# Gates of chunk and memory attention projected with the activations stationary, and turned back on VectorE and by GpSimd's transfers

## The chip, the core and the metric

One core of one Trainium2 chip runs the whole program. TensorE (PE) multiplies, VectorE (DVE) and ScalarE (ACT) do elementwise work, GpSimd (POOL) and SyncE (SP) mostly issue DMAs. The metric is device time in microseconds for one execution, the median of the runs. The kernel before takes 915.07 us (three runs, 915.05 to 915.77).

## The reference

Two layers of one mixer each; 256 rows of width 2048, all in f32. One input projection feeds three groups of heads, each group's output is multiplied by a SiLU gate, and one output projection follows.

```python
h = x @ w_in
a_q, a_k, a_v, a_z, b_q, b_k, b_v, b_z, b_lr, m_q, m_z = jnp.split(h, cuts, axis=-1)
y_a = chunk_band_attention(...)      # 8 heads of 128
y_b = rms_norm(gla_chunk_recurrence(...))   # 4 heads of 128
y_m = memory_attention(...)          # 4 heads of 128 over 256 memory rows
y = jnp.concatenate([y_a * silu(a_z), y_b * silu(b_z), y_m * silu(m_z)], axis=-1)
out = y @ w_out
x = layer_norm(ALPHA * x + out, ln_g, ln_b)
```

`a_z` has 1024 columns, `b_z` and `m_z` 512 each. The change touches `a_z` and `m_z`.

## The kernel before, in words

Every projection is cut into groups of 512 weight columns (four of 388 for the values). A group's weights come in eight pieces of 512 KB, called here pieces 0 to 7. Each f32 operand is used as the sum of a high and a low part, both stored as float32r, and of the four products the low times low is left out. `piece` (L128) issues the DMA of a piece on SP's queue, then `parts` (L115) makes its high part `wh` with a cast on ACT (L117) and its low part `wl` with a subtraction on DVE (L118). The buffers `raw`, `wh` and `wl` have four slots each, so the cast of a piece waits until PE has read the piece four before it.

There are two ways to multiply a group.

- `ws_group` (L250) keeps the weights stationary and streams the activations: for 128 rows of the contraction and 128 columns one matmul of 512 (high and low activations side by side) and one of 256. The result stands with its columns on the partitions. `total` (L261) adds the two halves.
- `as_group` (L273) keeps the activations stationary and streams the weights: per 128 rows of the contraction and each half `t` of the 256 rows three matmuls of 512. The result stands with the rows on the partitions, in one accumulator `acc` of two halves.

In a layer the order of the groups is: memory keys and values, gated linear attention's queries and keys, the values, the queries and keys of chunk attention, memory's queries, then the gates: `G_BZ` (L857, `as_group`), `G_AZ0`, `G_AZ1`, `G_MZ` (L864 to L876, `ws_group`), then four groups of the output projection, called here out 0 to out 3 (L908 to L927, `as_group`). Out 0 reads its activations `yq` in this order: gated linear attention at pieces 0 and 1, chunk attention's first four heads at pieces 2 and 3, its second four at 4 and 5, memory attention at 6 and 7.

The heads are generators. `tick` (L46) runs a step of one of them after every few matmuls of a group, and `finish` (L62) runs them to their end, so the order of PE's and SP's instructions is that in which the code is written and ticked. ACT, DVE and POOL are put in order by the build's scheduler, which gives `piece` a high priority. All five engines then work through their own list strictly in that order.

`turned` (L506) is a transposition that PE has no part in: DVE transposes blocks of 32 by 32 (L510), POOL writes them to HBM (`home`, L512, 256 KB), and four more DMAs of POOL read them back with the blocks exchanged (L514, 64 KB each, into `pT` or `yT`). The heads use it for their softmax, and `gla_turned` for the output of gated linear attention. Attention's outputs `yraw[1]` to `yraw[3]` have their columns on the partitions, as the result of `ws_group` has.

In the loop over `G_AZ0`, `G_AZ1` and `G_MZ` each of a group's two accumulators goes through ACT's and DVE's addition (`total`), SiLU on ACT (L870), then, when the group's heads are done, the product with `yraw` on DVE (L874) and the split into high and low (`x`).

Of the kernel before, what the change touches and what calls it, by code (L numbers as in the profile page):

```python
# [8 lines left out]
F32 = mybir.dt.float32  # L9
# [9 lines left out]
P = 128  # L19
# [17 lines left out]
def hybrid_trunk_kernel(  # L37
# [35 lines left out]
    def enter(name, bufs=1, **kw):  # L73
        return ctx.enter_context(tc.tile_pool(name=name, bufs=bufs, **kw))
# [8 lines left out]
    sm = enter("sm", 1)  # L83
    psd = enter("psd", 2, space=bass.MemoryType.PSUM)
    psa = enter("psa", 4, space=bass.MemoryType.PSUM)
    drm = enter("drm", 3, space=bass.MemoryType.DRAM)

    uid = [0]

    def nm(s):  # L90
        uid[0] += 1
        return f"{s}_{uid[0]}"
# [7 lines left out]
    def scratch(shape, dtype=F32):  # L100
        return sc.tile(shape, dtype, name=nm("sc"), tag="sc")
# [18 lines left out]
    def load_quarter(src):  # L120

        with tc.high_priority(AHEAD):
            raw = wp.tile([P, 4, T], F32, name=nm("raw"), tag="raw")
            x = operand()
            sp.dma_start(raw, src)
            parts(x[0], x[1], raw)
        return x

    def piece(src, n, kp=2, home=None):

        with tc.high_priority(AHEAD):
# [12 lines left out]
        return hi, lo  # L144
# [125 lines left out]
        mm(o, xl[:, j, ts], wh[:, kk], False, False)  # L270
        mm(o, xh[:, j, ts], wl[:, kk], False, kt == 15)

    def as_group(src, xq, n, kp=2, first=None):  # L273

        acc = psd.tile([P, 2, 512], F32, name=nm("acc"), tag="acc")
        for pc in range(16 // kp):
            if first is not None and pc % 2 == 0:
                xq.append(load_quarter(first[pc // 2]))
            w = piece(src[pc], n, kp)
            for kk in range(kp):  # L280
                for t in range(2):
# [209 lines left out]
    def gla_turned(yraw, ng, y):  # L491

        yT = []
        for par in range(2):
            yT.append(hd.tile([P, 4, P], F32, name=nm("yT"), tag=("gq", "gk")[par]))
            turned(yT[par], yraw[:, 2 * par:2 * par + 2].rearrange("p t d -> p (t d)"), P)
            yield 6
        for par in range(2):
            for t in range(2):
                for b in range(2):  # L500
                    hi, lo = (x.rearrange("p k (t a j) -> p k t a j", t=2, j=32)[:, b * 2 + par, t] for x in y[:2])
                    src = yT[par].rearrange("p a (t b j) -> p t b a j", t=2, j=32)[:, t, b]
                    act.activation(hi, src, AF.Copy, scale=ng[:, 0:1])
                    dve.scalar_tensor_tensor(lo, src, ng[:, 0:1], hi.bitcast(F32), op0=ALU.mult, op1=ALU.subtract)
            yield 1

    def turned(dst, src, n):

        blocks = scratch([P, 4, n])
        dve.transpose(blocks.rearrange("p b (g j) -> p g b j", j=32), src.rearrange("p (g b j) -> p g b j", b=4, j=32))  # L510
        home = drm.tile([P, 4, n], F32, name=nm("home"), tag=f"home{n}")
        pool.dma_start(home, blocks)  # L512
        for b in range(4):
            pool.dma_start(dst[b * 32:(b + 1) * 32], home[:, b].rearrange("(a i) n -> i a n", a=4))  # L514

    SCALE = P ** -0.5

    def a_head(h, load_bias, bias, q, k, asv, y):

        if h + 2 < 8:  # L520
            load_bias(h + 2)
        pb = bank()
        mm(pb[:, 0:128], q[:, 0:128], k[:, 0:128], True, True)
        mm(pb[:, 128:384], q[:, 128:256], k, True, True)
        s = scratch([P, 384])
        dve.scalar_tensor_tensor(s, pb[:, :384], SCALE, bias[h], op0=ALU.mult, op1=ALU.add)  # L526
        mx = small([P, 2], "mx", 4)
        zs = small([P, 2], "zs", 4)
        own = (slice(0, 128), slice(128, 384))
        for t in range(2):  # L530
            dve.tensor_reduce(mx[:, t:t + 1], s[:, own[t]], AX.X, ALU.max, negate=True)  # L531
        for t in range(2):
            act.activation(s[:, own[t]], s[:, own[t]], AF.Exp, bias=mx[:, t:t + 1], accum_out=zs[:, t:t + 1])  # L533
        dve.reciprocal(zs, zs)
        for t in range(2):
            dve.tensor_scalar(s[:, own[t]], s[:, own[t]], zs[:, t:t + 1], None, op0=ALU.mult)
        pT = tp.tile([P, 4, 96], F32, name=nm("pT"), tag="pT")
        turned(pT, s, 96)
        yield 9
        po = bank()  # L540
        v0 = 528 + h * P
        pv, pov = pT.rearrange("p a (g j) -> p g a j", j=32), po[:, :256].rearrange("p (t a j) -> p t a j", t=2, j=32)
        mm(pov, asv[:, 0, v0:v0 + P], pv[:, 0:2], True, False)
        mm(pov[:, 1], asv[:, 1, v0:v0 + P], pv[:, 2], False, True)
        act.copy(y, po[:, :256])
        yield 2

    def m_head(h, q, mk, mv, y):

        pb = bank()  # L550
# [18 lines left out]
        turned(pT, s.rearrange("p t m -> p (t m)"), 128)  # L569
# [12 lines left out]
        act.copy(y, po[:, :256])  # L582
        yield 2
# [187 lines left out]
    for l in range(L):  # L771
# [77 lines left out]
        for i, a, b in ws_group(w512[l, G_MQ], xq):  # L849
# [4 lines left out]
        waiting.extend(gens[-1])  # L854


        acc = as_group([[w512[l, G_BZ, h * 4 + pc // 2][:, pc % 2 * 512:pc % 2 * 512 + 512] for h in range(2)]  # L857
                        for pc in range(8)], xq, 512)
# [4 lines left out]
        waiting[:0] = gens[0]  # L863
        for i, g in ((1, G_AZ0), (2, G_AZ1), (3, G_MZ)):  # L864
            y = operand()
            gates = []
            for j, a, b in ws_group(w512[l, g], xq):
                sz = scratch([P, 2, T])
                total(sz, a, b)
                act.activation(sz, sz, AF.Silu)  # L870
                gates.append((j, sz))
            finish(gens[i])
            for j, sz in gates:
                dve.tensor_tensor(sz, sz, yraw[i][:, j:j + 2], op=ALU.mult)  # L874
                parts(y[0][:, j:j + 2], y[1][:, j:j + 2], sz)
            yq.append(y)  # L876
        finish(gens[0])


# [4 lines left out]
        for n in range(WO_N):  # L884
# [9 lines left out]
            if last and n == WO_N - 1:  # L894
# [23 lines left out]

                norm_last(accs, rest, stats, gb, rows, more)
                break  # L920
            acc = as_group(src, yq, 512)
            for t in range(2):
                add_residual(n, t, acc[:, t], stats)
            if last:
# [91 lines left out]
```

## Time and profile before

| | |
|---|---|
| profiled execution, its own time | 914.58 us |
| span of its instructions | 912.8 us, granted clock 0.998 |
| PE, DVE, ACT, POOL busy | 905.3, 605.2, 489.5, 99.0 us |
| DMA | 191.43 MB, mean 210 GB/s |
| gates of layer 0: G_AZ0 begins, out 0 begins | 293.43 and 365.27 us |

The profile names tiles without their numbers, output first: `acc<-x,wh` is a matmul that streams the activations against stationary weights, `acc<-wh,x` one that streams the weights. A row of the timeline has the start, the duration, the engine, the line, the operation, its tiles and shape, and in brackets how long the engine had been idle and what ended that. Rows of groups have the count, the busy sum, the mean of one in ns, and the idle time before them. A row of waits has the sum, the count and the longest. The ends of matmuls are modelled, so the spacing of their starts is the better measure.

### The profile page before, as it was taken

How to read it: one execution, taken by the hardware profiler on the slowest of the kernel's cores; microseconds unless marked ns; L12 is line 12 of the kernel's file. 1: busy time of each engine (PE TensorE's matmuls, PEld its weight loads, DVE VectorE, ACT ScalarE, POOL GpSimd, SP SyncE). 2: the span in 40 equal slices, each digit the busy share in tenths (PEclk: the TensorE clock that was granted, in tenths of full speed). 3: DMA queues.
4: the chain of work that ended last, by engine and by line, in shares of the span. 5: the costliest groups of instructions: out<-in, count | busy, mean ns of one | idle time of the engine just before them, and what ended most of it. 6: DMA issues, size and time to landing. Idle time of an engine off the chain costs nothing.

```text
span 912.8 us, 14367 instructions
## 1 busy us (share of the span) xinstructions
PE 905.3 (99%) x5404; PEld 796.2 (87%) x5404; DVE 605.2 (66%) x861; ACT 489.5 (54%) x714; POOL 99.0 (11%) x189
## 2 busy tenths in 40 slices
PE   9999999999999999999999999999999999999997
PEld 7889998998888888888888899889888888888885
DVE  6764478656576767655587676885756576776566
ACT  6654475474454666433476445754844465763340
POOL 1000000013031232000000000001121232420000
PEclk9999999999999999999999999999999999999999
DMA  8965865558575769766775466556575766696652
GB/s 300 341 198 167 298 222 167 161 198 248 184 223 177 240 218 273 217 197 193 225 256 167 146 203 204 186 156 212 181 246 186 217 207 218 204 294 207 195 162 92
DMA packets 76822, 191.43 MB, mean 210 GB/s; under 512 B 9545, under 2 KB 33481, under 8 KB 76497
## 3 DMA queue, kind: packets, MB, share of 16 engines
q1 hardware_dynamic: 69120, 173.30, 58.8%
q0 software_dynamic: 7488, 16.96, 6.5%
q8 instruction: 42, 0.69, 0.3%
q10 hardware_dynamic: 144, 0.26, 0.1%
q14 instruction: 28, 0.22, 0.1%
HBM read 182.06 MB, written 8.39 MB: 209 GB/s over the span
## 4 chain that ended last, share of the span: by engine, by line
PE 98%; DMA 0%; DVE 0%; ACT 0%; SPq 0%; issue 0%
PE acc L95 90%; PE bk L95 8%; DMA raw<-w 0%; PE bk L601 0%; PE bk L397 0%; SPq L178 0%; ACT res L757 0%; ACT wh L117 0%; DVE stats L742 0%; PE bk L344 0%; DVE res L741 0%; DVE res L693 0%; DVE mvt L696 0%; SPq L165 0%; PE bk L745 0%
## 5 line engine op out<-in xcount | busy, mean ns | idle before, releaser
L118 DVE TENSOR_TENSOR wl<-raw,wh 128x1024 fp32r<-128x1024 f32 (+3 forms) x321 | 369.8, 1154 | 227.2 <-ACT wh L117 226.0
L117 ACT CAST wh<-raw 128x1024 fp32r<-128x1024 f32 (+3 forms) x321 | 318.9, 994 | 324.7 <-PE acc L95 237.6
L95 PE MATMUL acc<-x,wh 128*128 128x512 f32 x1248 | 396.1, 399 | 0.5 <-ACT wh L117 0.5
L95 PE MATMUL acc<-wh,x 128*128 128x512 f32 (+2 forms) x1236 | 356.7, 370 | 0.2 <-ACT wh L117 0.2
L95 PEld LDWEIGHTS acc<-x,wl 128*128 128x128 f32 x1248 | 234.4, 188 | 55.2
L95 PEld LDWEIGHTS acc<-wh,x 128*128 128x128 f32 x1236 | 227.3, 188 | 27.6 <-ACT wh L117 0.5
L95 PE MATMUL acc<-x,wl 128*128 128x256 f32 x1248 | 245.7, 278 | 0.0
L95 PE MATMUL acc<-wl,x 128*128 128x512 f32 (+2 forms) x618 | 227.9, 369 | 0.0
L95 PEld LDWEIGHTS acc<-x,wh 128*128 128x128 f32 x1248 | 192.2, 189 | 2.5 <-ACT wh L117 0.7
L95 PEld LDWEIGHTS acc<-wl,x 128*128 128x128 f32 x618 | 116.2, 188 | 14.7 <-DVE wl L118 0.4
L514 POOL DMA_DIRECT2D pT<-home x96 | 52.6, 554 | 54.6 <-DMA home<-sc 33.4
L512 POOL DMA_DIRECT2D home<-sc x28 | 15.7, 561 | 361.6 <-DVE sc L510 357.9
L533 ACT ACTIVATE sc<-sc,mx 128x128 f32<-128x128 f32 (+1 forms) x32 | 14.3, 449 | 18.0 <-DVE mx L531 18.0
L526 DVE SCALAR_TENSOR_TENSOR sc<-bk,bias 128x384 f32<-128x384 f32 x16 | 8.7, 543 | 11.7 <-PE bk L95 11.7
L386 ACT ACTIVATE sc<-sc 128x512 f32<-128x512 f32 x12 | 7.6, 633 | 14.7 <-DVE sc L384 14.6
L510 DVE STREAM_TRANSPOSE sc<-sc 128x384 f32<-128x384 f32 (+1 forms) x24 | 14.9, 619 | 0.5
L304 POOL DMA_DIRECT2D gwraw<-gate_w x6 | 3.1, 524 | 106.0 <-PE bk L589 105.2
L118 DVE TENSOR_TENSOR x<-sc,x 128x512 fp32r<-128x512 f32 x20 | 13.5, 685 | 0.7 <-ACT x L117 0.7
L634 DVE SCALAR_TENSOR_TENSOR res<-res,acc 128x512 f32<-128x512 f32 x15 | 9.7, 684 | 5.4 <-PE acc L95 5.4
L118 DVE TENSOR_TENSOR x<-res,x 128x512 fp32r<-128x512 f32 (+2 forms) x14 | 10.5, 765 | 4.2 <-ACT x L117 4.2
L95 PE MATMUL bk<-qk,qk 128*128 128x128 f32 (+1 forms) x64 | 13.1, 327 | 0.0
L118 DVE TENSOR_TENSOR x<-raw,x 128x1024 fp32r<-128x1024 f32 x5 | 6.1, 1212 | 10.5 <-ACT x L117 10.5
(207 smaller groups left out, 586.1 us busy)
## 6 DMA issues: line engine op xcount, KB each, us to landing
raw<-w SPq DMA_DIRECT2D x214, 512.0 KB, 4.2
raw<-w SPq DMA_DIRECT2D x64, 388.0 KB, 3.2
raw<-w SPq DMA_DIRECT2D x83, 256.0 KB, 3.5
bias<-relw SPq DMA_DIRECT2D x16, 192.0 KB, 4.3
home<-sc POOLq DMA_DIRECT2D x16, 192.0 KB, 3.1
pT<-home POOLq DMA_DIRECT2D x64, 48.0 KB, 3.8
home<-sc POOLq DMA_DIRECT2D x12, 256.0 KB, 4.0
res<-xT SPq DMA_DIRECT2D x4, 512.0 KB, 5.1
```

Of the source, the lines that this page charges most:

```text
L95: pe.matmul(o, l, r, start=start, stop=stop, skip_group_check=True)
L117: act.copy(hi, src)
L118: dve.tensor_tensor(lo, src, hi.bitcast(F32), op=ALU.subtract)
L304: pool.dma_start(raw[i * 16:i * 16 + 16], gate_w[l])
L386: act.activation(dd, dd, AF.Abs)
L510: dve.transpose(blocks.rearrange("p b (g j) -> p g b j", j=32), src.rearrange("p (g b j) -> p g b j", b=4, j=32))
L512: pool.dma_start(home, blocks)
L514: pool.dma_start(dst[b * 32:(b + 1) * 32], home[:, b].rearrange("(a i) n -> i a n", a=4))
L526: dve.scalar_tensor_tensor(s, pb[:, :384], SCALE, bias[h], op0=ALU.mult, op1=ALU.add)
L533: act.activation(s[:, own[t]], s[:, own[t]], AF.Exp, bias=mx[:, t:t + 1], accum_out=zs[:, t:t + 1])
L634: dve.scalar_tensor_tensor(r, r, ALPHA, acc, op0=ALU.mult, op1=ALU.add)
```

## The change

The three groups `G_AZ0`, `G_AZ1` and `G_MZ` now go through `as_group`. Their weights lie in HBM as two halves of 256 columns, so a piece is fetched with two DMAs of 256 KB, as `G_BZ`'s already were (`halves`). The result has the rows on the partitions: ACT applies SiLU straight from the accumulator, in two instructions (L889), and `turned` brings it to columns on partitions: two transpositions, two writes to HBM, then eight loads into `zT`. The new generator `gated` waits until the heads are done and multiplies `zT` with `yraw`, in four instructions (L517), and splits the products in two. It is put among the running generators, and `as_group` of out 0 finishes it before the piece that reads its result (`need`: at pieces 2, 4 and 6). `turned` now takes several tiles and issues all writes before the first load. The pause in `gla_turned` is 2 then 6 ticks in place of 6 and 6.

```diff
-    def as_group(src, xq, n, kp=2, first=None):
+    def as_group(src, xq, n, kp=2, first=None, need={}):
...
+            finish(need.get(pc, ()))
             w = piece(src[pc], n, kp)
...
+    def gated(zT, yraw, heads, y):
+
+        while not all(h in done for h in heads):
+            yield 1
+        for j in range(0, 4, 2):
+            gz = scratch([P, 2, T])
+            for t in range(2):
+                z, o, r = (zT[:, t].rearrange("p a (k j) -> p k a j", j=32)[:, j:j + 2],
+                           *(x[:, :, t * P:(t + 1) * P].rearrange("p k (a j) -> p k a j", j=32) for x in (gz, yraw[:, j:j + 2])))
+                dve.tensor_tensor(o, z, r, op=ALU.mult)
+            parts(y[0][:, j:j + 2], y[1][:, j:j + 2], gz)
+
+    def turned(n, *todo):
+
+        homes = []
+        for _, src in todo:
+            blocks = scratch([P, 4, n])
+            dve.transpose(blocks.rearrange("p b (g j) -> p g b j", j=32), src.rearrange("p (g b j) -> p g b j", b=4, j=32))
+            homes.append(drm.tile([P, 4, n], F32, name=nm("home"), tag=f"home{n}"))
+            pool.dma_start(homes[-1], blocks)
+        for (dst, _), home in zip(todo, homes):
+            for b in range(4):
+                pool.dma_start(dst[b * 32:(b + 1) * 32], home[:, b].rearrange("(a i) n -> i a n", a=4))
...
         for i, g in ((1, G_AZ0), (2, G_AZ1), (3, G_MZ)):
-            y = operand()
-            gates = []
-            for j, a, b in ws_group(w512[l, g], xq):
-                sz = scratch([P, 2, T])
-                total(sz, a, b)
-                act.activation(sz, sz, AF.Silu)
-                gates.append((j, sz))
-            finish(gens[i])
-            for j, sz in gates:
-                dve.tensor_tensor(sz, sz, yraw[i][:, j:j + 2], op=ALU.mult)
-                parts(y[0][:, j:j + 2], y[1][:, j:j + 2], sz)
-            yq.append(y)
+            acc = as_group(halves(g), xq, 512)
+            yq.append(operand())
+            zT = hd.tile([P, 2, 4, P], F32, name=nm("zT"), tag="qk", bufs=4)
+            sz = [scratch([P, 512]) for _ in range(2)]
+            for t in range(2):
+                act.activation(sz[t], acc[:, t], AF.Silu)
+            turned(P, *((zT[:, t], sz[t]) for t in range(2)))
+            need[i * 2] = [gated(zT, yraw[i], gens[i], yq[i])]
+            active.extend((x, now[0] + 5) for x in need[i * 2])
         finish(gens[0])
...
-            acc = as_group(src, yq, 512)
+            acc = as_group(src, yq, 512, need=need if n == 0 else {})
```

Three places in the programs, where the order on ACT, DVE and POOL differs. The first is ACT in layer 0 at the end of `G_MZ`. Before, with the operands of the last memory head (`sc<-pT`), the last pieces of `G_MZ` (`wh_3653`, `wh_3683`) and pieces 0 and 1 of out 0 (`wh_3720`, `wh_3738`):

```order
L117 CAST wh_3653<-raw_3652 128x1024
L117 CAST sc_3551<-pT_3356 128x2x128 x2
L117 CAST wh_3683<-raw_3682 128x1024
L262 ACTIVATE sc_3587<-acc_3478 128x512
L582 COPY yr_1035<-bk_3579 128x256
L870 ACTIVATE sc_3587<-sc_3587 128x512
L117 CAST wh_3720<-raw_3719 128x1024
```

Now `wh_3686`, `wh_3704`, `wh_3722`, `wh_3740` are pieces 0 to 3 of out 0, `sc_3542` is the operand of the last memory head, and `acc_3451` is the accumulator of `G_MZ`:

```order
L117 CAST wh_3686<-raw_3685 128x1024
L598 COPY yr_1035<-bk_3577 128x256
L117 CAST wh_3704<-raw_3703 128x1024
L117 CAST wh_3722<-raw_3721 128x1024
L117 CAST sc_3542<-pT_3363 128x2x128 x2
L598 COPY yr_1035<-bk_3631 128x256
L117 CAST wh_3740<-raw_3739 128x1024
L889 ACTIVATE sc_3660<-acc_3451 128x512
```

The last head's operand has moved from ahead of the last piece of `G_MZ` to behind piece 2 of out 0; PE's last products of that head (`bk_3631`) still stand ahead of piece 7 of `G_MZ`.

The second is DVE in layer 1, where the low parts of memory attention's gated output are written. Before, the last write (`x_7771`) is ahead of the low part `wl_8144`, piece 6 of out 0:

```order
L118 TENSOR_TENSOR wl_8108<-raw_8106,wh_8107 128x1024
L874 TENSOR_TENSOR sc_7998<-sc_7998,yr_5329 128x512
L118 TENSOR_TENSOR wl_8126<-raw_8124,wh_8125 128x1024
L118 TENSOR_TENSOR x_7771<-sc_7998,x_7771 128x2x256
L118 TENSOR_TENSOR wl_8144<-raw_8142,wh_8143 128x1024
```

Now `wl_8114` is piece 7 of out 0, `wl_8144` and `wl_8162` are pieces 0 and 1 of out 1, and `x_7928` is that output:

```order
L118 TENSOR_TENSOR wl_8114<-raw_8112,wh_8113 128x1024
L517 TENSOR_TENSOR sc_8066<-zT_7929,yr_5305 128x2x128
L517 TENSOR_TENSOR sc_8071<-zT_7929,yr_5305 128x2x128
L118 TENSOR_TENSOR wl_8144<-raw_8142,wh_8143 128x1024
L118 TENSOR_TENSOR gbrow_7953<-gbrow_7951,gbrow_7952 2x1024
L118 TENSOR_TENSOR wl_8162<-raw_8160,wh_8161 128x1024
L517 TENSOR_TENSOR sc_8066<-zT_7929,yr_5305 128x2x128
L517 TENSOR_TENSOR sc_8071<-zT_7929,yr_5305 128x2x128
L118 TENSOR_TENSOR x_7928<-sc_8066,x_7928 128x2x256
L118 TENSOR_TENSOR x_7928<-sc_8071,x_7928 128x2x256
```

The last write stood behind piece 5 of out 0 and now stands behind piece 1 of out 1, four pieces later. In layer 0 the two high casts (`x_3658` on ACT) stand behind `wh_3868`, the same piece 1 of out 1.

The third is POOL in layer 0 around the end of `G_MZ`. Before there are only the transfers of the heads, the gated linear attention's (`yT`) and the rows of the norm (`gb`, broadcasts of 256 KB):

```order
L514 DMA pT_3356<-home_3359 32x4x128 x4
L514 DMA yT_3458<-home_3461 32x4x128 x4
L890 DMA gb_4023<-ln_g 128x512
L891 DMA gb_4023<-ln_b 128x512
L820 MEMSET lr_5009 128x256
```

Now the gates' transfers stand between them (`zT_3430` of `G_AZ1`, `zT_3659` of `G_MZ`):

```order
L530 DMA zT_3430<-home_3437 32x4x128 x4
L530 DMA zT_3430<-home_3441 32x4x128 x4
L836 MEMSET lr_4985 128x256
L527 DMA home_3666<-sc_3664 128x512
L906 DMA gb_3999<-ln_g 128x512
L907 DMA gb_3999<-ln_b 128x512
L527 DMA home_3670<-sc_3668 128x512
L530 DMA zT_3659<-home_3666 32x4x128 x4
L530 DMA zT_3659<-home_3670 32x4x128 x4
```

Two broadcasts have come to stand between the two writes of `G_MZ`'s gates, and the loads follow both.

More of the change, by code (lines that the diff above doesn't have):

```diff
@@ L85, in hybrid_trunk_kernel @@
     psa = enter("psa", 4, space=bass.MemoryType.PSUM)
-    drm = enter("drm", 3, space=bass.MemoryType.DRAM)
+    drm = enter("drm", 6, space=bass.MemoryType.DRAM)
     uid = [0]
@@ L495, in gla_turned @@
             yT.append(hd.tile([P, 4, P], F32, name=nm("yT"), tag=("gq", "gk")[par]))
-            turned(yT[par], yraw[:, 2 * par:2 * par + 2].rearrange("p t d -> p (t d)"), P)
-            yield 6
+            turned(P, (yT[par], yraw[:, 2 * par:2 * par + 2].rearrange("p t d -> p (t d)")))
+            yield 2 + 4 * par
         for par in range(2):
@@ L505, in gla_turned @@
             yield 1
[L507 to L514, printed above, removed]
+    def gated(zT, yraw, heads, y):
[18 more added lines that the diff above has]
+                pool.dma_start(dst[b * 32:(b + 1) * 32], home[:, b].rearrange("(a i) n -> i a n", a=4))
     SCALE = P ** -0.5
@@ L537, in a_head @@
         pT = tp.tile([P, 4, 96], F32, name=nm("pT"), tag="pT")
-        turned(pT, s, 96)
+        turned(96, (pT, s))
         yield 9
@@ L568, in m_head @@
         pT = hd.tile([P, 4, 128], F32, name=nm("pT"), tag="qe" if h % 2 else "gb_")
-        turned(pT, s.rearrange("p t m -> p (t m)"), 128)
+        turned(128, (pT, s.rearrange("p t m -> p (t m)")))
         yield 7
@@ L854, in hybrid_trunk_kernel, with halves @@
         waiting.extend(gens[-1])
-        acc = as_group([[w512[l, G_BZ, h * 4 + pc // 2][:, pc % 2 * 512:pc % 2 * 512 + 512] for h in range(2)]
-                        for pc in range(8)], xq, 512)
+        def halves(g):
+            return [[w512[l, g, h * 4 + pc // 2][:, pc % 2 * 512:pc % 2 * 512 + 512] for h in range(2)] for pc in range(8)]
+        acc = as_group(halves(G_BZ), xq, 512)
         finish(gens[0])
@@ L863, in hybrid_trunk_kernel @@
         waiting[:0] = gens[0]
+        need = {}
         for i, g in ((1, G_AZ0), (2, G_AZ1), (3, G_MZ)):
-            y = operand()
-            gates = []
-            for j, a, b in ws_group(w512[l, g], xq):
-                sz = scratch([P, 2, T])
-                total(sz, a, b)
-                act.activation(sz, sz, AF.Silu)
-                gates.append((j, sz))
-            finish(gens[i])
-            for j, sz in gates:
-                dve.tensor_tensor(sz, sz, yraw[i][:, j:j + 2], op=ALU.mult)
-                parts(y[0][:, j:j + 2], y[1][:, j:j + 2], sz)
-            yq.append(y)
+            acc = as_group(halves(g), xq, 512)
[7 more added lines that the diff above has]
+            active.extend((x, now[0] + 5) for x in need[i * 2])
         finish(gens[0])
```

## The prediction

> **What bounds the kernel now.** I read the page first (busy times, the chain that ended last), then the waits, then the timeline of PE, ACT and POOL where the changed groups end.
>
> ```profile
> span 912.8 us, 14367 instructions
> ...
> PE 905.3 (99%) x5404; PEld 796.2 (87%) x5404; DVE 605.2 (66%) x861; ACT 489.5 (54%) x714; POOL 99.0 (11%) x189
> ...
> PE 98%; DMA 0%; DVE 0%; ACT 0%; SPq 0%; issue 0%
> ```
>
> PE is the whole chain. The waits say how little it is held up, and who waits for whom instead:
>
> ```profile
> ACT wh L117 <- PE acc L95: 237.6, 170, 2.1
> ...
> ACT wh L117 <- DMA raw<-w: 15.3, 20, 3.2
> ...
> PE bk L95 <- DVE eps L770: 1.1, 1, 1.1
> ...
> PE acc L95 <- ACT wh L117: 0.7, 2, 0.5
> ```
>
> ACT waits for PE to free a weight slot, seldom for a weight. So a microsecond of PE's work counts fully, and a wait of PE is never made up. The change is worth what it does to PE's rate, less any new wait of PE.
>
> **PE's rate: -3.1 us.** The end of the memory gates (weights stationary) and out 0 (activations stationary):
>
> ```profile
> 357.61 0.63 PE L95 MATMUL acc<-x,wh 128*128 128x512 f32 x2
> ...
> 364.57 0.63 PE L95 MATMUL acc<-x,wh 128*128 128x512 f32 x2
> ...
> 365.27 0.62 PE L95 MATMUL acc<-wh,x 128*128 128x512 f32 x2
> ...
> 381.60 0.62 PE L95 MATMUL acc<-wh,x 128*128 128x512 f32 x2
> ...
> 388.40 0.62 PE L95 MATMUL acc<-wh,x 128*128 128x512 f32 x2
> ```
>
> Both ways stream 1536 columns per step: twice 512 and twice 256, or thrice 512. From 357.61 to 364.57 are ten steps of 0.696 us, from 381.60 to 388.40 ten of 0.680. A group has 32 steps, so it goes from 22.27 to 21.76 us, and six groups give 6 x 0.51 = 3.1 us. A piece is four steps, 2.72 us. Out 0 begins at 365.27, which I call T0, and its piece 6 at 381.60, T0 + 16.33: then the memory gates' output must be there.
>
> **What the other engines pay: nothing, with cover.** Durations of one, by shape:
>
> ```profile
> L118 DVE TENSOR_TENSOR wl<-raw,wh 128x1024 fp32r<-128x1024 f32 x248 | 302.2, 1221 | 164.1 <-ACT wh L117 163.1
> ...
> L117 ACT CAST wh<-raw 128x1024 fp32r<-128x1024 f32 x248 | 259.8, 1049 | 238.4 <-PE acc L95 163.0 <-issue 51.1 <-DMA raw<-w 8.4
> ...
> L118 DVE TENSOR_TENSOR x<-sc,x 128x512 fp32r<-128x512 f32 x20 | 13.5, 685 | 0.7 <-ACT x L117 0.7
> ...
> L263 DVE SCALAR_TENSOR_TENSOR sc<-acc,sc 128x512 f32<-128x512 f32 x19 | 13.0, 682 | 0.0
> ...
> L117 ACT CAST x<-sc 128x512 fp32r<-128x512 f32 x20 | 12.0, 616 | 1.3 <-DVE sc L609 1.3
> ...
> L874 DVE TENSOR_TENSOR sc<-sc,yr 128x512 f32<-128x512 f32 x12 | 8.2, 687 | 3.5 <-ACT sc L870 3.5
> ...
> L870 ACT ACTIVATE sc<-sc 128x512 f32<-128x512 f32 x12 | 7.6, 630 | 4.6 <-DVE sc L263 4.5
> ...
> L118 DVE TENSOR_TENSOR sc<-pT,sc 128x256 fp32r<-128x256 f32 x16 | 6.0, 420 | 3.1 <-ACT sc L117 3.1
> ...
> L117 ACT CAST sc<-pT 128x256 fp32r<-128x256 f32 x16 | 5.7, 403 | 5.6 <-DMA pT<-home 5.6
> ...
> L510 DVE STREAM_TRANSPOSE sc<-yr 128x512 f32<-128x512 f32 x4 | 2.7, 687 | 0.0
> ...
> L487 ACT ACTIVATE sc<-acc 128x512 f32<-128x512 f32 x4 | 2.2, 598 | 0.0
> ```
>
> Per group ACT loses its share of the addition (two, about 0.59 each) and reads the accumulator in its SiLU (0.60 for 0.63); DVE loses two additions (0.68) and two products (0.69), and gains two transpositions (0.69) and four products of 256 (0.42, the nearest row is the subtraction of that size): +0.3 us. Both have 4 us and more to spare per group, since they wait for PE. The 48 pieces that now come as two DMAs are covered by four slots of 2.72 us; without that cover each piece could cost its landing of some 4 us. POOL gains 12 writes and 48 loads: 60 x 0.56 = 33 us on an engine that is busy 11%. The rows of the norm that queue behind them on POOL are wanted only after out 0. DVE's products that wait for `zT` hold the weights' low parts behind them, under the same cover of four slots. What counts is when the loads land:
>
> ```profile
> 316.83 0.56 POOL L512 DMA_DIRECT2D home<-sc  x1 [12.51 <-DVE sc L510]
> 320.66 2.18 POOL L514 DMA_DIRECT2D yT<-home  x4 [3.27 <-DMA home<-sc]
> ...
> 338.94 1.12 POOL L512 DMA_DIRECT2D home<-sc  x2
> ...
> 344.87 2.21 POOL L514 DMA_DIRECT2D pT<-home  x4 [3.74 <-DMA home<-sc]
> ```
>
> ```profile
> home<-sc POOLq DMA_DIRECT2D x6, 256.0 KB, 4.1
> pT<-home POOLq DMA_DIRECT2D x16, 64.0 KB, 4.8
> sc<-ln_g POOLq DMA_DIRECT2D x4, 256.0 KB, 5.3
> ```
>
> (The second view is the DMAs by issue at the same gates in layer 1, 741 to 831 us, with the median to landing.) From a write's issue to the first load went 3.83 us at 316.83, and 5.4 for the second write at 338.94, which had broadcasts beside it.
>
> **Where PE will wait: +9.7 us.** Three times, since the scheduler has put operands of PE behind a weight piece whose slot PE itself frees only just before it needs them. The slot rule in the trace, with the memory gates' last high cast of before:
>
> ```profile
> 371.70 0.61 ACT L117 CAST x<-sc 128x512 fp32r<-128x512 f32 x1
> ...
> 378.90 1.05 ACT L117 CAST wh<-raw 128x1024 fp32r<-128x1024 f32 x1 [1.67 <-PE acc L95]
> 381.57 1.05 ACT L117 CAST wh<-raw 128x1024 fp32r<-128x1024 f32 x1 [1.62 <-PE acc L95]
> ```
>
> The cast at 381.57 begins as PE goes from piece 5 to 6: piece 1 of out 1 takes the slot of piece 5. Before, the gates were cast at 371.70, ten microseconds early.
>
> A, layer 0, last memory head: +2.9. PE wants the head's operand between pieces 6 and 7 of the gates, and its cast stands behind piece 2 of out 0, whose slot is piece 6's. From the end of piece 6: the cast of the piece 1.05, two casts of the head 0.4 each less overlap, PE gets the high part at 1.8; DVE makes the piece's low part 1.1 to 2.3, then the head's two, 0.8; PE's third product starts at 3.1 and not at 0.24. Bounds: 1.8 if the low part were free, 3.3 with nothing overlapping.
>
> B, layer 0, piece 6 of out 0: +3.0. ACT casts piece 3 of out 0 until T0 + 1.1, then SiLU to 1.7 and 2.3. DVE transposes at 2.3 to 3.0 and, after two products of the group before, at 3.9 to 4.6. POOL writes half 1 at 3.05 and half 2, behind two broadcasts, at 5.0. Half 1 is read from 6.9 (3.83 later) to 9.1, half 2 from 10.4 (5.4 later) and lands 1.65 + 4.8 after, at 16.9. Products to 17.7, the high cast from 17.4 (behind piece 1 of out 1) to 18.0; DVE makes that piece's low part 17.7 to 18.9, then the gates' to 19.6. PE's second product needs it at 16.6. Bounds: 2.8 by the order alone, if everything has landed by 16.4; 6.2 if the loads take the slowest of `yT`, 8.0:
>
> ```profile
> DMA to landing us min/median/max: 2.2/4.4/8.0
> ```
>
> [...]
>
> C, layer 1, the same place: +3.8. Here DVE has even the second half's products behind piece 1 of out 1: its cast 16.4 to 17.4, its low part to 18.65, the products to 19.5, the gates' high cast 19.1 to 19.7, the low part to 20.4, against 16.6. The loads land by 17.7 (half 1 from 6.9, the last pair of half 2 only when the first of half 1 have landed, at 12.3 to 12.9, + 4.8), so they are hidden. Bounds: 3.8 and, with the same 8.0, 6.2.
>
> The sum against the profiled execution: 914.58 - 3.1 + 2.9 + 3.0 + 3.8 = 921.2. The median of the runs lies 0.5 above that execution (915.07), so I say 921.5.
>
> **The rivals.** *Hidden (faster).* If the chain's last write came before T0 + 16.3 in both layers and the head's operand in time, only the rate would be left: 915.07 - 3.1 = 912.0. For it speaks the slack before (371.70 against 381.60) and a first write read after 3.83 us; against it the order, which puts each of the three behind the slot that PE frees last. It decides whether ACT and DVE reach those rows before PE ends the piece.
>
> *Late transfers.* Each layer gets 3 MB more around here, where the DMA engines are this busy (layer 1, last gates and out 0):
>
> ```profile
> 786.00:809.00 23.00, 23.00 (x137) 20.25 (x136) 19.14 (x27) 16.74 (x26) 11.15 (x21) 1.00 0.95 284
> 809.00:831.00 22.00, 22.00 (x107) 18.49 (x106) 14.76 (x21) 12.72 (x20) 2.14 (x4) 1.00 0.84 270
> 906.00:912.70 6.70, 1.69 (x6) 0.98 (x6) 1.36 (x3) 1.38 (x2) 0.00 (x0) 0.80 0.45 157
> ```
>
> With the upper bounds of B and C: 921.5 + 3.2 + 2.4 = 927.1. For it: shares of 0.95 and 0.84 before anything is added. Against: broadcasts that fell into those windows now wait behind the loads.
>
> *Weights come short.* 1 MB at 284 GB/s is 3.5 us; if none of it fits beside the weights at the last gates of each layer, 921.5 + 7 = 928.5. Against: slots hold 11 us.
>
> *The clock drops.* Wait C leaves PE without work for 3.4 us. The last row above is the only stretch with a long idle PE, and its clock is 0.80: a loss of 0.20 x 6.7 = 1.3 us, so 922.8. [...] Before has no gap in its middle that could show it.
>
> **How the numbers follow.** Forecast (919.5 to 924) 0.64; late transfers 0.20; clock 0.05; weights short 0.03; hidden 0.06; waits that just eat the gain 0.02. The low end, 918.5, is the forecast without A; the high end, 928, holds most of the late case. A measurement tells 0.2%, 1.8 us, from no change: faster 0.06, same 0.02, slower 0.92.
>
> **What would show it.** Right: `acc<-x,wh` of 512 falls from 1248 by 384; steps of 0.68 us in the gates; PE's waits name `sc` of L117/L118 once, 3 us, ahead of piece 7 of the gates, and `x` of L117/L118 twice, 3 to 4 us, at piece 6 of out 0; POOL near 132 us busy. Wrong: no wait there (hidden), waits named after DMAs with loads over 6 us (late), waits on `wh` (weights), or a clock under 1.00 around out 0. What most easily makes it wrong is the time at which half 2 lands.

## The result, and the profile after

The changed kernel takes 931.58 us (median of four runs, 931.31 to 932.76), the kernel before 915.06 us (914.59 to 915.77): ratio 1.0185, 95% interval 1.0173 to 1.0197. It is slower, as forecast, but by 16.5 us and not by 6.4, and 3.6 us above the range's upper end. The profiled execution took 931.75 us with a span of 929.9 us, 17.1 more than before.

Of the page, the span, the busy times and the group that the weight-stationary steps make:

```profile
span 929.9 us, 14207 instructions
...
PE 909.5 (98%) x5212; PEld 790.3 (85%) x5212; DVE 605.7 (65%) x873; ACT 483.6 (52%) x702; POOL 131.6 (14%) x249
...
L95 PE MATMUL acc<-x,wh 128*128 128x512 f32 x864 | 275.4, 400 | 0.2 <-ACT wh L117 0.2
```

`acc<-x,wh` fell from 1248 to 864 and POOL rose to 131.6 us, as the edit makes it, and the gates' steps are 0.68 us apart (349.55 and 350.23 us). The mean granted clock fell from 0.998 to 0.991. PE's waits, longest in total first:

```profile
PE acc L95 <- ACT x L117: 8.9, 2, 5.8
PE bk L95 <- ACT sc L117: 1.7, 2, 1.5
PE bk L95 <- DVE sc L118: 1.7, 2, 0.9
...
PE acc L95 <- DVE x L118: 0.9, 2, 0.6
```

The two waits on `x` are places B and C of the prediction. The two on `sc` are place A and, not foreseen, the same wait for the last head but one. None stands on `wh` for more than 0.3 us. The places on PE's timeline, in order of time (the last head but one, A, B, C):

```profile
354.69 0.50 PE L95 MATMUL bk<-sc,mv 128*128 128x256 f32 x2 [0.22 <-ACT sc L117]
...
361.89 0.39 PE L95 MATMUL acc<-wl,x 128*128 128x512 f32 x1
363.80 0.50 PE L95 MATMUL bk<-sc,mv 128*128 128x256 f32 x2 [1.52 <-ACT sc L117]
365.12 0.75 PE L95 MATMUL bk<-sc,mv 128*128 128x256 f32 x4 [0.81 <-DVE sc L118]
365.70 0.63 PE L95 MATMUL acc<-wh,x 128*128 128x512 f32 x2
...
390.71 0.79 PE L95 MATMUL acc<-wh,x 128*128 128x512 f32 x1 [5.79 <-ACT x L117]
392.13 0.80 PE L95 MATMUL acc<-wh,x 128*128 128x512 f32 x1 [0.63 <-DVE x L118]
...
393.15 1.06 PE L95 MATMUL acc<-wh,x 128*128 128x512 f32 x2
...
394.43 1.06 PE L95 MATMUL acc<-wh,x 128*128 128x512 f32 x2
...
397.80 0.62 PE L95 MATMUL acc<-wh,x 128*128 128x512 f32 x2
...
842.70 0.39 PE L95 MATMUL acc<-wl,x 128*128 128x512 f32 x1
846.24 0.50 PE L95 MATMUL acc<-wh,x 128*128 128x512 f32 x1 [3.15 <-ACT x L117]
846.97 0.50 PE L95 MATMUL acc<-wh,x 128*128 128x512 f32 x1 [0.22 <-DVE x L118]
...
851.88 0.62 PE L95 MATMUL acc<-wh,x 128*128 128x512 f32 x2
```

At B and C something follows the wait: a step starts every 1.28 us (393.15, 394.43) where it should every 0.68. The windows around B and C show why (span, PE, PEld, DVE, ACT and POOL busy with their counts, then the granted clock, the DMA share and GB/s):

```profile
385.00:390.00 5.00, 0.00 (x0) 0.00 (x0) 2.31 (x5) 1.04 (x1) 0.00 (x0) 0.70 0.76 239
390.00:395.00 5.00, 3.66 (x8) 2.60 (x9) 2.68 (x5) 1.14 (x2) 1.10 (x2) 0.50 0.48 144
395.00:400.00 5.00, 5.00 (x19) 4.05 (x18) 1.23 (x1) 1.17 (x2) 0.00 (x0) 0.78 0.21 75
...
845.00:850.00 5.00, 3.53 (x10) 2.60 (x11) 2.17 (x5) 1.14 (x2) 1.07 (x3) 0.78 0.97 309
850.00:855.00 5.00, 5.00 (x21) 4.04 (x20) 2.92 (x4) 3.05 (x3) 1.34 (x3) 0.88 0.73 160
```

At B the clock falls while PE still idles (0.70 from 385 to 390 us, where PE has nothing to do), and behind each of these waits it is at half for some microseconds (0.50 from 390 to 395 us, and at C 0.50 from 848 to 850).

Why B is twice as long as forecast, on GpSimd's queue (`home` are the two writes, `gb` two broadcasts of norm rows, `zT` the loads):

```profile
371.64 0.56 POOL L527 DMA_DIRECT2D home<-sc  x1 [6.20 <-DVE sc L517]
372.28 0.56 POOL L906 DMA_DIRECT2D gb<-ln_g  x1
372.83 0.54 POOL L907 DMA_DIRECT2D gb<-ln_b  x1
373.36 0.54 POOL L527 DMA_DIRECT2D home<-sc  x1
375.67 2.20 POOL L530 DMA_DIRECT2D zT<-home  x4 [1.77 <-DMA home<-sc]
381.37 2.17 POOL L530 DMA_DIRECT2D zT<-home  x4 [3.50 <-DMA home<-sc]
```

Half 1 was read 4.03 us after its write was issued, half 2 8.01 us after (373.36 to 381.37). The landings tell the same: half 1's write took 3.4 us, the two broadcasts behind it 6.1 and 7.4, half 2's write 7.7, its four loads 6.5. DVE's products with half 2 then began at 389.58, released by the last load.

PE's time, worked out from these rows. Out 0 begins at 368.44 in layer 0, so piece 6 is due at 384.76. Its first product came 5.95 us late, its second 1.19 more, 7.1 in all; its sixth step, due at 388.16, came at 397.80, 9.6 late, so 2.5 us went to the clock. (Some 0.3 of the 7.1 is the half clock as well: the first product lasts 0.79 us there and 0.50 in layer 1.) In layer 1 piece 6 is due at 842.93: 3.3 and 0.5 late, 3.8 in all; the sixth step 5.5 late, 1.7 for the clock. Around the last head PE needed 3.81 us (361.89 to 365.70) and around the last but one 2.58 (354.08 to 356.66), where a run without these waits, `e5_rows`, needs 0.96 (360.80 to 361.76): 2.9 and 1.6 late.

| term | predicted, us | measured, us |
|---|---|---|
| rate of six groups | -3.1 | -2.6 (all that run `e9_both` gains) |
| last head but one | 0 | +1.6 |
| A, last head | +2.9 | +2.9 |
| B, layer 0, wait | +3.0 | +7.1 |
| C, layer 1, wait | +3.8 | +3.8 |
| half clock behind B and C | 0 (rival: 1.3) | +2.5, +1.7 |
| sum | +6.6 | +17.0 |

The span grew by 17.1.

### The profile page after: what moved, and what is told of

The parts are those of the page before. It is cut to its first block, busy times and chain, and to the rows that moved or that the text cites. A ratio compares the mean times of both kernels' runs of the same rounds, so it can differ in the third digit from the quotient of the medians.

```text
span 929.9 us, 14207 instructions
## 1 busy us (share of the span) xinstructions
PE 909.5 (98%) x5212; PEld 790.3 (85%) x5212; DVE 605.7 (65%) x873; ACT 483.6 (52%) x702; POOL 131.6 (14%) x249
## 4 chain that ended last, share of the span: by engine, by line
PE 57%; DVE 0%; ACT 0%; issue 0%; DVEq 0%
PE acc L95 52%; PE bk L95 4%; PE bk L617 0%; ACT wh L117 0%; DVE x L118 0%; ACT res L773 0%; ACT x L117 0%; DVE stats L758 0%; PE bk L398 0%; DVE res L757 0%; DVE sc L517 0%; DVE res L709 0%; DVE mvt L712 0%; PE bk L761 0%; ACT nparts L117 0%
## 5 line engine op out<-in xcount | busy, mean ns | idle before, releaser
L95 PE MATMUL acc<-wh,x 128*128 128x512 f32 (+2 forms) x1620 | 479.5, 377 | 10.0 <-ACT x L117 8.9
L95 PEld LDWEIGHTS acc<-wh,x 128*128 128x128 f32 x1620 | 300.5, 189 | 54.6 <-ACT x L117 9.8
L95 PE MATMUL acc<-wl,x 128*128 128x512 f32 (+2 forms) x810 | 304.4, 376 | 0.0
L95 PE MATMUL acc<-x,wh 128*128 128x512 f32 x864 | 275.4, 400 | 0.2 <-ACT wh L117 0.2
L95 PEld LDWEIGHTS acc<-x,wl 128*128 128x128 f32 x864 | 162.3, 188 | 38.2
L95 PEld LDWEIGHTS acc<-wl,x 128*128 128x128 f32 x810 | 153.1, 189 | 22.6 <-DVE wl L118 0.8
L95 PE MATMUL acc<-x,wl 128*128 128x256 f32 x864 | 170.2, 278 | 0.0
L95 PEld LDWEIGHTS acc<-x,wh 128*128 128x128 f32 x864 | 133.5, 189 | 2.0 <-ACT wh L117 0.4
L530 POOL DMA_DIRECT2D zT<-home x48 | 26.2, 552 | 15.9 <-DMA home<-sc 7.7
L525 DVE STREAM_TRANSPOSE sc<-sc 128x512 f32<-128x512 f32 (+1 forms) x36 | 22.9, 645 | 1.7 <-ACT sc L889 1.2
L517 DVE TENSOR_TENSOR sc<-zT,yr 128x256 f32<-128x256 f32 x24 | 8.8, 416 | 7.2 <-DMA zT<-home 7.2
```

The costliest lines, as they stand in the source:

```text
L95: pe.matmul(o, l, r, start=start, stop=stop, skip_group_check=True)
L517: dve.tensor_tensor(o, z, r, op=ALU.mult)
```

## The experiments

Each run is compared with runs of the kernel before on the same chip (their median was 914.87 to 914.96 us).

### Which groups cost it

`e1_mem_old` keeps the memory gates with weights stationary, `e2_mem_only` the chunk gates. Both put the old code in front of the new (here and below, `...` stands for lines left out):

```
+            if g == G_MZ:        # e2_mem_only: g != G_MZ
+                y = operand()
+                gates = []
+                for j, a, b in ws_group(w512[l, g], xq):
...
+                yq.append(y)
+                continue
             acc = as_group(halves(g), xq, 512)
```

> The chunk gates are projected as in the changed kernel, the memory gates with weights stationary as before; nothing is left out. Theory (the time went into PE's waits at piece 6 of out 0, and the half clock behind them): both places lose their wait, 9.6 us in layer 0 and 5.5 in layer 1, two groups give their 0.5 us back, and the waits for the last two memory heads stay: 931.6 - 15.1 + 1.0 = 917.5 us. Rival (the weights that come as two transfers, or the turning as such, slow the kernel everywhere): four of the six groups are still turned, so some two thirds of the loss stay, about 926.

Measured: 918.11 us, ratio 1.0039 (1.0024 to 1.0054). PE has no wait on `x` any more, the clock is 1.00 in every window from 335 to 420 us, and both heads' waits are there (1.9 us on ACT's and 1.6 on DVE's `sc`). The theory holds; the four turned groups and the two heads' waits together cost 3.2 us.

> Only the memory gates are turned; the chunk gates are as before; nothing is left out. Theory (the order of the casts makes the waits at piece 6 of out 0, and the other groups' transfers lengthen the one of layer 0): against the kernel before, -1.0 for the rate of two groups, +3.0 to 3.8 for the wait of layer 0, +3.8 for that of layer 1, and 1.7 to 2.5 of half clock behind each: 915.1 + 9.2 to 10.8, 924 to 926 us. If the other turned groups have no part in the lateness of layer 0 (wait 7.1), 928 to 929 us. Rival (the chunk gates cost as much): under 920 us.

Measured: 927.92 us, ratio 1.0146 (1.0131 to 1.0161). The waits at B and C:

```profile
385.95 0.79 PE L95 MATMUL acc<-wh,x 128*128 128x512 f32 x1 [3.22 <-ACT x L117]
387.37 0.79 PE L95 MATMUL acc<-wh,x 128*128 128x512 f32 x1 [0.63 <-DVE x L118]
...
842.10 0.50 PE L95 MATMUL acc<-wh,x 128*128 128x512 f32 x1 [3.15 <-ACT x L117]
842.82 0.80 PE L95 MATMUL acc<-wh,x 128*128 128x512 f32 x1 [0.22 <-DVE x L118]
```

The memory gates alone make B and C. B's wait is between the two theories, 4.6 us by the same reckoning as above, and here the half clock (0.51 from 385 to 390 us, 0.75 from 840 to 845) costs 2.3 and 1.6: 914.96 - 1.0 + 4.6 + 2.3 + 3.8 + 1.6, and 1.3 for one wait for a head (0.8 of it idle), are 927.6. C does not depend on the chunk gates at all. Here the two writes of the memory gates stand side by side on GpSimd's queue (369.45 us), no broadcast between them, and DVE's products with half 2 (384.83) follow a weight piece's low part without waiting for a load: B, too, is then made by the order alone, as C is.

### Is it when the output is wanted?

`e4_late` moves the product that reads the memory gates back by six pieces:

```
...
+            if n == 0:
+                part = as_group(src, yq, 512, need={k: need[k] for k in (2, 4)}, pcs=range(6)), src
+                continue
+            if n == 1:
+                acc1 = as_group(src, yq, 512, pcs=range(6))
+                acc = as_group(part[1], yq, 512, need={6: need[6]}, acc=part[0], pcs=(6, 7))
...
+                acc = as_group(src, yq, 512, acc=acc1, pcs=(6, 7))
```

> All six groups are turned; the last two pieces of out 0, which read the memory gates' output, come after the first six of out 1, 16 us later; nothing is left out. Theory (the waits are a matter of when the output is wanted): the waits at piece 6 of out 0 and the half clock behind them go, the waits for the last two memory heads stay: 931.6 - 15.1 = 916.5 us. Rival (the time is lost to transfers or weights wherever the product stands): 925 us or more.

Measured: 917.17 us, ratio 1.0027 (1.0016 to 1.0038). All six groups are turned and B and C are gone. What is left over the kernel before are the heads' waits, waits for weights (2.0 us on `wh`, 0.7 before) and, in the profiled execution, a clock that fell behind A, where PE had idled only 1.5 and 0.8 us:

```profile
365.00:367.00 2.00, 1.19 (x7) 0.98 (x7) 1.05 (x3) 0.00 (x0) 0.31 (x1) 0.84 0.91 248
367.00:369.00 2.00, 2.00 (x6) 1.57 (x6) 0.76 (x2) 0.38 (x1) 0.00 (x0) 0.50 1.10 258
369.00:371.00 2.00, 2.00 (x8) 1.60 (x7) 0.00 (x0) 0.02 (x1) 0.00 (x0) 0.81 0.60 191
```

That is a loss of 0.16 x 2 + 0.50 x 2 + 0.19 x 2 = 1.7 us.

### Does the clock fall because PE idles?

`e6_warm` gives PE something to do while it waits:

```
...
             finish(need.get(pc, ()))
+            for i in range(warm if pc == 6 and need else 0):
+                if i == 0:
+                    idle = bank()
+                mm(idle, xq[0][0][:, 0, :P], xq[0][2][:, 0], True, True)
...
-            acc = as_group(src, yq, 512, need=need if n == 0 else {})
+            acc = as_group(src, yq, 512, need=need if n == 0 else {}, warm=(24, 13)[l])
```

> The changed kernel with 24 (layer 0) and 13 (layer 1) matmuls of 512 columns whose result nobody reads ahead of piece 6 of out 0: 5.4 and 2.9 us of work, in the place of an idle PE. Theory (the clock falls because PE idles): the waits end at the same time as before, the half clock behind them goes, 2.5 and 1.7 us: 927.4 us. Rival (the clock falls for another reason, such as the work that follows or a fixed window): no less than 931 us.

Measured: 929.27 us (926.56 to 930.95), ratio 1.0153 (1.0131 to 1.0175). In the profiled execution the clock stays up at B and C and falls behind A (the last row):

```profile
385.00:390.00 5.00, 5.00 (x24) 4.14 (x23) 1.90 (x3) 2.10 (x2) 0.61 (x2) 1.00 0.76 229
390.00:395.00 5.00, 3.89 (x16) 2.72 (x15) 3.10 (x5) 1.14 (x2) 1.10 (x2) 1.00 0.50 138
...
845.00:850.00 5.00, 4.55 (x19) 3.20 (x18) 1.69 (x4) 1.97 (x3) 1.56 (x3) 1.00 0.87 327
...
367.00:369.00 2.00, 2.00 (x7) 1.54 (x6) 0.66 (x2) 0.00 (x0) 0.00 (x0) 0.50 1.03 221
```

The matmuls nobody reads take the half clock away from both places, which is what the theory said of the mechanism: with PE busy over the same stretch (its product at B still came 5.8 us late, at 392.60) the clock stays up. The time fell by 2.3 us and not by 4.2; 1.7 of the profiled execution's time is the drop behind A (0.96, 0.50 and 0.69 in the three stretches of 2 us from 365 to 371), which the changed kernel's profiled execution did not have.

`e11_warm_head` is `e6_warm` with six more of them at A:

```
+        if h == 3 and l == 0:
+            idle = bank()
+            for i in range(6):
+                mm(idle, xq[0][0][:, 0, :P], xq[0][2][:, 0], True, True)
```

> The run with idle matmuls ahead of piece 6 of out 0, with six more of them (1.4 us) ahead of the last memory head's product with the values in layer 0, where PE waited 1.5 and 0.8 us. Theory (the clock also falls at that shorter wait, in some executions, and costs 1.7 us; that is the scatter of that run, 926.6 to 931.0): the clock is 1.00 from 360 us on, and the time is 927 us with less scatter. Rival (a gap as short as that has no part in the clock): a clock under 1.00 shows again between 365 and 371 us in some executions, and the scatter stays.

Measured: 928.61 us (925.14 to 929.47), ratio 1.0143 (1.0123 to 1.0164). The profiled execution, the one of 925.14 us, has a clock of 1.00 in every window from 350 to 400 us and from 830 to 860 us, but the scatter stayed. So the expectation failed: the drop behind A is not all of the scatter. The mean clocks of the four executions, 0.996 to 0.998, are worth 0.002 x 928 = 1.9 us of the 4.3 between them. The build's scheduler also placed GpSimd's writes differently in this kernel (half 2 right behind half 1), so it is not a pure repeat. What the other executions lost their time to stays open, since only one execution of a kernel is profiled.

### What made half 2 late

`e5_rows` issues all broadcasts of norm rows behind the memory gates' last load, `e10_two_rows` only the two that stood between the writes of layer 0:

```
...
+            with tc.issue_after(turn.ins):      # e10_two_rows: only for n == 2 of layer 0
-            pool.dma_start(g, ln_g[l:l + 1, columns(n)].to_broadcast([P, 512]))
-            pool.dma_start(b, ln_b[l:l + 1, columns(n)].to_broadcast([P, 512]))
+                pool.dma_start(g, ln_g[l:l + 1, columns(n)].to_broadcast([P, 512]))
+                pool.dma_start(b, ln_b[l:l + 1, columns(n)].to_broadcast([P, 512]))
```

> The changed kernel, with the broadcasts of the norm's rows (eight in layer 0, six in layer 1) issued on GpSimd's queue behind the last loads of the memory gates; the planner answers by putting the last two memory heads' casts one or two pieces earlier and the two transpositions of the memory gates side by side; nothing is left out. Theory (the broadcasts between the two writes made half 2 late, and the heads' casts stood behind weight pieces): the waits for the heads go (2.9 + 1.1), the wait of layer 0 falls from 7.1 to the 3.0 that the order alone makes, layer 1 keeps its 5.5: 931.6 - 4.0 - 4.1 = 923.5 us, and 921 if the shorter gap leaves the clock alone. Rival (half 2 is late for the weights' sake): the wait of layer 0 stays over 6 us, 927 us or more.

Measured: 924.28 us, ratio 1.0093 (1.0066 to 1.012). No wait on `sc` is left, and B's is 2.17 and 0.93 us, though the half clock still followed it (0.50 from 385 to 390 us):

```profile
383.17 0.49 PE L95 MATMUL acc<-wh,x 128*128 128x512 f32 x1 [2.17 <-ACT x L117]
384.59 0.79 PE L95 MATMUL acc<-wh,x 128*128 128x512 f32 x1 [0.93 <-DVE x L118]
```

> The changed kernel, with only the two broadcasts of layer 0 that stood between the two writes of the memory gates issued behind the last loads instead; ACT's order is the changed kernel's, DVE's differs in one place (the first two products stand ahead of a weight piece's low part); the last two memory heads keep their waits; nothing is left out. Theory (these two broadcasts made half 2 late): half 2 is written at 372.3 instead of 373.4, takes 4 us instead of 8 and has been read by about 385, so the wait of layer 0 falls from 7.1 us to the 3.0 that the order makes: 931.6 - 4.1 = 927.5 us, and 925.0 where the clock stays up as well. Rival (half 2 is late for the weights' sake, whatever stands before it): 930.5 us or more.

Measured: 927.43 us, ratio 1.0145 (1.0128 to 1.0162). GpSimd's queue and PE's timeline of this run:

```profile
372.94 0.56 POOL L527 DMA_DIRECT2D home<-sc  x1 [0.70 <-DVE sc L525]
375.74 4.42 POOL L530 DMA_DIRECT2D zT<-home  x8 [2.25 <-DMA home<-sc]
```

```profile
386.66 0.50 PE L95 MATMUL acc<-wh,x 128*128 128x512 f32 x1 [1.71 <-ACT x L117]
388.09 0.50 PE L95 MATMUL acc<-wh,x 128*128 128x512 f32 x1 [0.92 <-DVE x L118]
```

With the two broadcasts out of the way half 2's write lands after 4.8 us in place of 7.7 (its loads, the last four of the eight, begin at about 377.9, 5.0 us after it was issued), the eight loads follow each other without a gap, and B's wait is 2.6 us by these rows instead of 6.4; by the reckoning of the result section (out 0 begins at 368.47) PE is 3.1 us late instead of 7.1, near the 3.0 that I had put on B. Two broadcasts of 256 KB cost this kernel some 4 us. Whether they did it by their place in the queue or by sharing the DMA engines is not shown. The profiled execution is the fastest of the four, 925.26 us, and in it the clock did not fall behind B at all:

```profile
385.00:390.00 5.00, 2.42 (x9) 1.79 (x10) 3.63 (x6) 1.95 (x3) 1.06 (x2) 1.00 0.76 240
```

The other three, at 926.84 to 929.42 us, had mean clocks of 0.991 and 0.992 for this one's 0.996.

`e7_pack` is the rival cause, the packets of the weights:

```
...
-                G_BZ: 5120, G_AZ0: 3072, G_AZ1: 3584, G_MZ: 6160}
+                G_BZ: 5120}
+        for g, c in {G_AZ0: 3072, G_AZ1: 3584, G_MZ: 6160}.items():
+            w512[l, g] = pack(wi[:, c:c + 512])
...
-            acc = as_group(halves(g), xq, 512)
+            acc = as_group(w512[l, g], xq, 512)
```

> The changed kernel, with the weights of the three turned groups laid out as those of out 0 are: one transfer of 512 KB with runs of 4 KB per piece instead of two of 256 KB with runs of 1 KB; every instruction of ACT, DVE, POOL and PE stands where it stood; nothing is left out. Theory A (the broadcasts and the order make the waits): within 1 us of 931.6. Theory B (the 21,700 added packets fill the DMA engines, so that weights and half 2 come late): the wait for the last head but one goes (1.1) and the wait of layer 0 falls from 7.1 towards 3.0: 926.4 us, less if the clock stays up.

Measured: 930.84 us, ratio 1.017 (1.0154 to 1.0186); B's wait is 5.16 us ahead of the first product (5.79 in the changed kernel), and half 2's write, issued at 374.33, was read from 382.71, 8.4 us later. Theory A: the form in which the weights come is not what makes half 2 late. That the time is so close to 931.6 is partly chance: in the profiled execution the clock fell behind A (0.71 from 365 to 370 us), as it did not in the changed kernel's, and did not fall behind C, as it did there, although PE waited the same 3.15 and 0.22 us (847.07 and 847.79 us):

```profile
845.00:850.00 5.00, 2.71 (x11) 2.02 (x12) 2.99 (x5) 1.14 (x2) 1.80 (x4) 1.00 0.93 316
```

### What the order alone makes

`e3_order` changes no instruction and no transfer; it moves the memory gates' casts and low parts ahead of those of piece 1 of out 1:

```
...
-            w = piece(src[pc], n, kp)
+            with ExitStack() as order:
+                for ins in behind if pc else ():
+                    order.enter_context(tc.issue_after(ins.ins))
+                w = piece(src[pc], n, kp)
...
```

(`behind` holds the last cast and low part of the memory gates, and is passed for out 1 alone.)

> The changed kernel, with only the issue order of ACT and DVE altered at out 0: the high casts and low parts of the memory gates' output stand ahead of those of piece 1 of out 1, in both layers, instead of behind them; nothing is left out. Theory (layer 1's wait is made by the order, layer 0's by half 2's loads): layer 0 keeps its 7.1 us of wait but for the low part's 0.6; layer 1's loads have landed by about 843.7, so its wait falls from 3.4 us to about 1.7, and with so short a gap the half clock behind it goes (1.7): 931.6 - 0.6 - 1.7 - 1.7 = 927.6 us. Rival (both waits are the loads'): no less than 931 us.

Measured: 931.49 us (925.61 to 934.23), ratio 1.0172 (1.0131 to 1.0214). Layer 0 did as expected (5.7 us ahead of the first product, and the 0.63 ahead of the second gone). In layer 1 the expectation failed: PE still waits there, on DVE's products, which now wait for the load:

```profile
846.17 0.51 PE L96 MATMUL acc<-wh,x 128*128 128x512 f32 x1 [2.33 <-ACT x L118]
846.89 0.50 PE L96 MATMUL acc<-wh,x 128*128 128x512 f32 x1 [0.22 <-DVE x L118]
```

```profile
845.04 0.76 DVE L520 TENSOR_TENSOR sc<-zT,yr 128x256 f32<-128x256 f32 x2 [0.67 <-DMA zT<-home]
```

In the changed kernel they did not wait for it. They follow the low part of piece 1 of out 1 without a pause:

```profile
843.98 1.23 DVE L118 TENSOR_TENSOR wl<-raw,wh 128x1024 fp32r<-128x1024 f32 x1 [0.36 <-ACT wh L117]
845.12 0.75 DVE L517 TENSOR_TENSOR sc<-zT,yr 128x256 f32<-128x256 f32 x2
```

So the order makes C in the changed kernel, and the same 3.15 us return in `e2_mem_only`, `e5_rows` and `e7_pack`. The landing stands close behind it: with the order out of the way it holds PE for 2.33 us, and only 0.8 is gained. A wait of 2.33 and 0.22 us was again followed by the half clock: the window from 845 to 850 us stands at 0.76, and steps are 1.28 us apart there (848.61 and 849.89). The time of the profiled execution, 931.61 us, did not fall: its clock also fell behind A (0.66 from 365 to 370 us), which cost some 1.7 us that the changed kernel's did not pay. Why the four executions lie 8.6 us apart is not shown.

### Both kernels beaten

`e9_both` is `e4_late` with the edit of `e5_rows`.

> The run with the last two pieces of out 0 put behind six of out 1, and the run with the broadcasts behind the loads, in one kernel; nothing is left out. Theory (the waits for the last two memory heads are all that the first of these left over): only the rate of six groups is left of the change, 915.0 - 3.1 = 911.9 us, with up to 1 us on top for small waits. Rival (turning costs elsewhere, too): 914 us or more.

Measured: 912.31 us (911.97 to 912.66), ratio to the kernel before 0.9971 (0.996 to 0.9981). PE waits for none of these operands any more. Its longest wait, 1.1 us at the program's start, is one that the kernel before has too, and the only one for a weight is this:

```profile
PE acc L95 <- ACT wh L117: 0.2, 1, 0.2
```

The eight loads of the memory gates run in a row here as well. 914.87 - 912.31 = 2.6 us is what the activations-stationary form is worth here when its result is in time, together with what the two moves bring along; the expectation of 911.9 was 0.4 us off.

## Why the prediction was wrong

**Right.** The direction, and its reason: PE's gain is small and fixed, and new waits of PE outweigh it. The rate (-3.1 against -2.6). A, to the tenth: the last head's cast stands behind a weight piece whose slot PE frees late. `e5_rows` moved that cast and the wait went. The places of B and C, and the names that PE would wait for. C, with its reason: out 0 of layer 1 begins at 826.61, so DVE's low part of piece 1 begins at T0 + 17.4 and its products with half 2 at T0 + 18.5, as forecast, the loads hidden before them. How closely they were hidden, by 0.8 us, only `e3_order` showed. Of half 2's last two loads, which I let wait for the landing of the first, one did: it was issued at 839.56, T0 + 12.95, after 0.70 us of waiting for a `zT` load. POOL's 33 us (131.6 busy against 99.0) cost nothing on POOL: none of PE's waits ends on it.

**Wrong: the transfer term of B.** The step was "half 2, behind two broadcasts, at 5.0", read "5.4 later" and landing "at 16.9". The write was issued when I said (373.36 is T0 + 4.9). It was read 8.0 us later, not 5.4, and DVE's products came only at T0 + 21.1. I took the 5.4 from a write with broadcasts beside it and the 8.0 only as a bound for the loads; it was the write that took 8.0, and the last loads took some 6.5 (from 383.0 to 389.5), not 4.8. `e10_two_rows` shows that the two broadcasts were the cause: moved, they give 4 us back. At B this is the rival that I called late transfers, with 7.1 us instead of its 6.2; at C, where that rival has 6.2 as well, it did not come true. What I set against it, that broadcasts now wait behind the loads, did not hold for the two that stand between the writes.

**Wrong: the clock's chance and place.** I gave it 0.05, in one window, although my own forecast put a wait of 3 to 4 us at B and at C. The row that I had, an idle PE with a clock of 0.80, should have made it part of the sum, once at each wait. I put it at nothing, and it cost 2.5 and 1.7 us. (The 1.3 us of the rival counted the low clock over all 6.7 us of that row, of which PE worked 1.69.)

**Wrong, small: the cover of the weights.** "Four slots of 2.72 us" did not hold around the last two heads, where the DMA share was 1.10 and 1.02 (345 to 350 and 350 to 355 us). ACT waited for weights there, and the cast of the last head but one came behind them:

```profile
348.41 1.05 ACT L117 CAST wh<-raw 128x1024 fp32r<-128x1024 f32 x1 [3.47 <-DMA raw<-w]
350.86 1.05 ACT L117 CAST wh<-raw 128x1024 fp32r<-128x1024 f32 x1 [1.40 <-DMA raw<-w]
...
353.94 0.70 ACT L117 CAST sc<-pT 128x256 fp32r<-128x256 f32 x2
```

1.6 us, on no line of mine. In `e5_rows`, with the broadcasts behind the loads, ACT waits for no weight between 344 and 366 us; since the scheduler moved casts as well there, that the broadcasts held these weights up is not shown.

One sum is off without consequence: 921.2 and 0.5 are 921.7, not 921.5.

## What to carry to other kernels

A result that turns up in another layout through memory is late by two transfers, and these are priced with what is issued around them (half 2 was read 8.0 us after its write was issued behind two broadcasts, 5.0 after without them): ask what is issued between the write and the next one, and move it behind. Ask also what limit stands behind the one that you remove: taking the order away at C gave 0.8 us of 3.15, since the loads came next. Where the late result is read matters more than how it is made; six pieces of other work between, and the broadcasts behind the loads, turned 16.5 us of loss into 2.6 of gain. And a wait of TensorE in the middle of dense work is priced with the half clock that may follow it, here 1.6 to 2.5 us on top where it was worked out.

## What the runs showed of the hardware

The clock can fall after much shorter waits than B's 5.79 and 0.63 us. That a short gap leaves it up, as the expectation of `e3_order` has it, was my own estimate, which no run had shown. An idle time of 2.33 and 0.22 us (`e3_order`, layer 1) was followed by half clock (0.76 from 845 to 850 us, with steps 1.28 us apart), and so was 1.5 and 0.8 us with 0.5 us of matmuls between (A; 0.50 from 367 to 369 us in `e4_late` and `e6_warm`).

The length of such a wait does not decide by itself. The same wait at A was followed by the drop in four of seven profiled executions (`e3_order` 0.66 and `e7_pack` 0.71 from 365 to 370 us, `e4_late` and `e6_warm` 0.50 from 367 to 369) and not in three (the changed kernel, `e1_mem_old` and `e10_two_rows`, 1.00). The 3.15 and 0.22 us of C were followed by it in the changed kernel (0.78 from 845 to 850 us), `e2_mem_only`, `e5_rows` and `e10_two_rows` (0.75, 0.66 and 0.66 from 840 to 845), and not in `e7_pack` (1.00 from 845 to 855). At B 2.17 and 0.93 us were in `e5_rows` (0.50 from 385 to 390 us), 1.71 and 0.92 were not in `e10_two_rows` (1.00). What decides between them no run here shows. One drop cost 2.5 and 1.7 us in the changed kernel (B and C), 2.3 and 1.6 in `e2_mem_only`, and 1.7 at A in `e4_late`.
